# Layer 0 of a two-layer encoder on one core: attention softmax in spaced steps, the short conv's weights two units earlier, the first block modulated first, two plain units of the output projection, and large tiles at multiples of 64 bytes

## The chip, the cores and the metric

The kernel runs on one core of one Trainium2 chip. Its engines are TensorE (PE, matrix products, with its weight loads shown as PEld), VectorE (DVE), ScalarE (ACT), GpSimd (POOL) and SyncE (SP), which issues all transfers here. They share an on-chip memory (SBUF) and the accumulators of TensorE (PSUM). The metric is the device time of one execution in microseconds (us), lower is better.

## What is computed

A two-layer encoder on 256 positions of width 2048, all in float32:

```python
for l in range(2):
    mod = (silu(c) @ w_mod[l] + b_mod[l])            # 2048 x 12288 per layer
    shift_m, scale_m, gate_m, shift_f, scale_f, gate_f = mod in six parts of 2048
    h = layer_norm(x) * (1.0 + scale_m) + shift_m
    proj = h @ w_in[l]
    uv, q_c, kv_c, k_r, sb, sc, sh, ag = split(proj)  # widths 1024, 384, 256, 64, 512, 512, 512, 1024
    y_a = gmlp_mixer(uv, ...)                         # A: chunked spatial gating
    y_b = mla_mixer(q_c, kv_c, k_r, ...)              # B: latent attention, 4 heads, rotary key
    y_c = sb * causal_dwconv3(sc * sh)                # C: short gated conv
    y_d = silu(layer_norm(causal_dwconv31(glu(ag))))  # D: conv module, 31 taps
    y = concatenate([y_a, y_b, y_c, y_d]) @ w_out[l]
    x = layer_norm(ALPHA * x + (1.0 + gate_m) * y, ...)
    h = layer_norm(x) * (1.0 + scale_f) + shift_f
    y = conv_ffn(h, ...)                              # 2048 -> 2 x 5632 -> 2048
    x = layer_norm(ALPHA * x + (1.0 + gate_f) * y, ...)
```

## The kernel before

**Precision and pools.** Most large products are done in a faster format: ACT casts a weight tile to a high part `whi` (L382), DVE subtracts it from the raw one `wraw` to give a low part `wlo` (L383), activations are split in the same way (L402), and three products (high x high, low x high, high x low) take the place of one. Such weights are "split". In layer 0 the input projection and the later chunks of `w_out` use "plain" float32 weights `wexact` instead, which go straight from the transfer into a product, on more TensorE time and no ACT or DVE time. Tiles come from pools of a few buffers each.

**Order.** The Python program emits instructions in an order of its own, and a scheduler then orders each engine's queue by data, buffers and manual dependencies. `stream` (L331) loads one unit of weights, emits the products of the unit before, calls `pump` and takes `bg` steps from the list `background`. A `phase` sets how many modulation steps `pump` emits for one unit (`RATES`), and `STEPS` sets how many background steps there are. `None` entries in `background` are steps that emit nothing.

**Modulation.** `mod` is a matrix times one vector, done on DVE: each of its steps takes 1 MB of `w_mod` and one instruction over 128x2048 (L188 `wmod<-wmod,crep`, or L198 `macc<-wmod,cact,macc` for a gate). The first two of layer 0 (shift and scale) are made block by block in `first_mod_of`: a block is 128 of the 2048 channels, two such products, a small sum (`mod`, L1407) and one ACT instruction on `hF`, the transposed normalised input. The other ten come from the stream of steps through `pump`.

**Layer 0's mixers.** `normed_T` normalises `x` with two powers on POOL (L141, `rs_in`) and writes `hF` with 32 transposes (`ps_xT`, L1390). `by_blocks` then goes through the 16 blocks of 128 channels, as each is modulated, with the D, U and V columns, next the B columns (latents of the attention) and at last the C columns (short conv). `mix_d` puts the 31 taps of conv D into `background`: four ACT scalings `scaled` (L842) and one DVE addition (L843) each, then `norm_d`: mean over channels, centring (L862), variance, power on POOL (`rd`, L876), a diagonal `dgD` (L882), and TensorE's `ps_rD` that spreads it. `attend` turns the latents `lat` by transposes (`ps_q`, `ps_kv`, L1000), scales them on ACT into `qg` (L1006, L1009), makes the rotary key (`kc`, L1012, and the `rope` copies), the queries and keys with `wq` and `wkv`, the scores and softmax (L1084 to L1121), and the product with the values.

**Output projection.** `out_proj` takes 2048 output columns in three chunks, `CHUNKS = ((0, 1024), (1024, 512), (1536, 512))`, and the 16 row blocks of `w_out` in units; in the first chunk a unit is two row blocks. `o` are its accumulators; the rows come in the order a, b, c, d of the mixers' outputs `ya` to `yd`. In layer 0 the second and third chunk are plain, the first is split.

Of the kernel before, what the change touches and what calls it, by code (L numbers as in the profile page):

```python
# [35 lines left out]
    dict(B=1.2, C=2.4, out=1.6, up=0.7, down=0.7),  # L36
    dict(D=1.0, U=0.0, V=0.0, B=0.0, C=0.0, E=0.9, out=0.6, up=0.3, down=0.7),
# [3 lines left out]
    dict(B=1, C=4, up=2),  # L41
    dict(U=7, B=4, C=4, E=8, up=2),
]

# [38 lines left out]
def encoder_kernel(ctx: ExitStack, tc: tile.TileContext, A: dict, consts: bass.AP, out: bass.AP):  # L83
# [56 lines left out]
    def power(o, i):  # L140
        pool.tensor_tensor(out=o, in0=i, in1=mhalf[:, : i.shape[1]], op=ALU.pow)  # L141
# [6 lines left out]
    par = keep.tile([P, PARAMS], F32, name="par")  # L148
# [31 lines left out]
    MOD = {}  # L180
    order_dep = mybir.DependencyInfo(mybir.DependencyClass.NoSync, mybir.DependencyReason.DATA)

    def mod_block(l, m, kt, col):

        raw = raw_tile("wmod")
        c0 = m * D + kt * P
        nc.sync.dma_start(out=raw, in_=A["w_mod"].take(D, lambda a: a[l, :, c0 : c0 + P].T))
        i = dve.scalar_tensor_tensor(  # L188
            out=raw, in0=raw, scalar=1.0, in1=crep, op0=ALU.mult, op1=ALU.mult, accum_out=col
        )  # L190
        held(i, "mod")

# [8 lines left out]
    def gate_rows(l, m, acc):  # L201
# [34 lines left out]
        return [lambda q=q: part(q) for q in range(5)]  # L236
# [94 lines left out]
    def stream(load, products, bg=0, mods=True):  # L331
# [4 lines left out]
        if mods:  # L336
            pump()
# [201 lines left out]
    def run(g):  # L539
        units, load, products, end, bg = g  # L540
        for u in range(units):
            stream(lambda: load(u), lambda item, u=u: products(item, u), bg)
            pending.extend(postponed)
            postponed.clear()
# [3 lines left out]
    last_norm = [None, None]  # L548

    def rstd_of(stats, name, want_nmr):  # L550
# [4 lines left out]
        power(r[:, 0:1], r[:, 0:1])  # L555
# [31 lines left out]
    def out_proj(l, w, src, order, gate_of, name, post_g, post_b, before, then, plain=(), bg=0):  # L587
# [111 lines left out]
        for c0, width in CHUNKS:  # L699
# [11 lines left out]
            def load_unit(u, c0, width, nk, units, last):  # L711
# [3 lines left out]
                exact = c0 in plain  # L715
                parts = weights(w, kt, nk, c0, width, exact, spare)
                s4 = src[kt // 4]
# [24 lines left out]

            for u in range(units):
                stream(lambda: load(u), lambda item, u=u, unit=unit: unit(item, u), bg if c0 == 0 else 1, not last)

            def done(state=state, c0=c0, nk=nk, last=last):
# [7 lines left out]
                if last:  # L754
                    drain_background()
                for t in range(2):
# [14 lines left out]
    def mixers(l, w_in, Y, hF=None, first_mod=None):  # L771
# [7 lines left out]
        CLB = lambda j: pm[:, 149 + j : 150 + j]  # L779

# [35 lines left out]
        def conv_d(glu):  # L816
# [16 lines left out]
            def taps(k):  # L833
# [7 lines left out]
                for j in range(4):  # L841
                    act.activation(out=t[:, j, :n], in_=glu[:, j, :n], func=AF.Copy, scale=CW(k, j))  # L842
                dve.tensor_tensor(out=yd[:, :, 30 - k :], in0=yd[:, :, 30 - k :], in1=t[:, :, :n], op=ALU.add)  # L843
# [10 lines left out]
            background.append(lambda: norm_d(yd))  # L854

        def norm_d(yd):
            Y["d"] = slot("yd").rearrange("p (j s) -> p j s", j=4)
            ps = ms_tile("ps_mean")
            for j in range(4):
                mm(ps[:, :S], ones, yd[:, j, :], j == 0, j == 3)  # L860
            for j in range(4):
                dve.scalar_tensor_tensor(  # L862
                    out=yd[:, j, :], in0=ps[:, :S], scalar=-1.0 / W_G, in1=yd[:, j, :], op0=ALU.mult, op1=ALU.add
                )
            sq = [tmp_tile("sqD0"), tmp_tile("sqD1")]
            for b in range(2):
                act.activation(
                    out=sq[b].rearrange("p (j s) -> p j s", j=2), in_=yd[:, 2 * b : 2 * b + 2, :], func=AF.Square
                )
            ps = ms_tile("ps_var")  # L870
            for t in range(2):
                for j in range(4):
                    o = (j % 2) * S + t * P
                    mm(ps[:, t : t + 1], sq[j // 2][:, o : o + P], ones[:, 0:1], j == 0, j == 3)
            rd = smallp.tile([P, 4], F32, tag="rd", name="rd")
            dve.tensor_scalar(  # L876
                out=rd[:, 0:2], in0=ps[:, 0:2], scalar1=1.0 / W_G, scalar2=LN_EPS, op0=ALU.mult, op1=ALU.add
            )
            power(rd[:, 2:4], rd[:, 0:2])
            dg = tmp_tile("dgD")  # L880
            for t in range(2):
                dve.tensor_scalar(  # L882
                    out=dg[:, t * P : (t + 1) * P], in0=ident, scalar1=rd[:, 2 + t : 3 + t], scalar2=None, op0=ALU.mult
                )
            ps = ms_tile("ps_rD")
            mm(ps[:, :S], ones, dg[:, :S], True, True)
            for j in range(4):
                dve.tensor_tensor(out=yd[:, j, :], in0=yd[:, j, :], in1=ps[:, :S], op=ALU.mult)
            for j in range(4):
                act.activation(out=Y["d"][:, j, :], in_=yd[:, j, :], func=AF.Silu, scale=CG(j), bias=CLB(j))  # L890

# [60 lines left out]
        def mix_b(wide, narrow):  # L952
# [38 lines left out]
            postponed.append(lambda: attend(WQ, WKV, lat, q01, rr))  # L991

        def attend(WQ, WKV, lat, q01, rr):
# [32 lines left out]
            act.copy(rope[64:128, 3, :], ps[64:128, :S])  # L1026

            qn = slot("qn").rearrange("p (j s) -> p j s", j=4)
            for b in range(2):
# [5 lines left out]
                act.copy(qn[:, 2 * b : 2 * b + 2, :], ps.rearrange("p (j s) -> p j s", j=2))  # L1035
            for b in range(2):
# [11 lines left out]
            for b in range(2):  # L1048
# [11 lines left out]
                act.copy(kn[:, 2 * b : 2 * b + 2, :], ps.rearrange("p (j s) -> p j s", j=2))  # L1060
# [514 lines left out]
```

## Time and profile before

| what | value |
|---|---|
| three runs | 2245.35, 2253.36, 2249.52 us; median 2249.52 |
| profiled execution | 2243.58 us; span in the trace 2241.8 us |
| mean granted TensorE clock | 0.996 |
| busy: PE / weight loads / DVE / ACT / POOL | 2196.2 / 1801.8 / 1722.7 / 1097.4 / 29.2 us |
| read from device memory | 600.01 MB, 269 GB/s over the span |
| layer 0: first D product; first C products; end of C; end of `w_out`'s first chunk | 25.09; 204.80; about 304; about 364 us |

The profile is of one execution. A row of the timeline has start, duration, engine, source line, operation, output and inputs, shapes and count, and in brackets how long the engine was idle ahead of it and what released it. A slice has the busy time of each engine with its number of instructions, the clock granted to TensorE, the DMA engines' busy share and the data rate. In a row of groups the busy total and the mean in ns stand behind the bar, and then the idle time ahead.

### The profile page before, as it was taken

The page shows a single profiled execution, that of the slowest core. Times are in us where ns is not written, and L with a number is a line of the kernel's source. Part 1 is how long each engine was busy: PE and PEld are TensorE (multiplying, and loading weights), DVE is VectorE, ACT ScalarE, POOL GpSimd, SP SyncE. Part 2 cuts the span into 40 slices and gives each one's busy share as a digit, 9 for nine tenths or more (in the row PEclk, how much of TensorE's full clock was granted, in tenths as well). Part 3 has the DMA queues.
Part 4 walks back from the last instruction along what each step waited for, and adds up shares of the span by engine and source line. Part 5 has one row for each costly group of instructions (what it writes and reads, how often), then busy time and mean ns, then how long its engine had stood idle before and what let it go on. Part 6 is the DMA issues. An engine that isn't in the chain of part 4 may idle for free. (4 is left out here: it accounts for less than half of the span.)

```text
span 2241.8 us, 28321 instructions
## 1 busy us (share of the span) xinstructions
PE 2196.2 (98%) x10852; PEld 1801.8 (80%) x10852; DVE 1722.7 (77%) x2203; ACT 1097.4 (49%) x1683; POOL 29.2 (1%) x38
## 2 busy tenths in 40 slices
PE   8999989999999999999999999999999999999997
PEld 5876865488888888888877988868888888888886
DVE  5658887698988888988968987867775566565776
ACT  3136431555545454545556544555555555454453
POOL 0000000000000000000000000000000000000000
PEclk9999999999999999999999999999999999999999
DMA  9998879598988889888766656866665555555554
GB/s 393 408 359 314 318 295 417 227 338 312 329 322 312 334 314 329 316 321 329 288 240 247 211 173 238 295 221 244 244 228 186 188 188 190 189 193 199 188 190 148
DMA packets 93746, 603.96 MB, mean 269 GB/s; under 512 B 10533, under 2 KB 10661, under 8 KB 28581
## 3 DMA queue, kind: packets, MB, share of 16 engines
q1 hardware_dynamic: 93610, 602.15, 73.2%
q8 instruction: 85, 1.39, 0.2%
q14 instruction: 51, 0.42, 0.1%
HBM read 600.01 MB, written 2.10 MB: 269 GB/s over the span
## 5 line engine op out<-in xcount | busy, mean ns | idle before, releaser
L382 ACT CAST whi<-wraw 128x1024 fp32r<-128x1024 f32 (+1 forms) x612 | 638.0, 1046 | 693.0 <-PE g_c L111 208.1
L383 DVE TENSOR_TENSOR wlo<-wraw,whi 128x1024 fp32r<-128x1024 f32 (+1 forms) x612 | 736.0, 1215 | 287.0 <-ACT whi L382 280.5
L111 PE MATMUL v_c<-hT,whi 128*128 128x512 f32 x1408 | 490.4, 392 | 0.0
L111 PE MATMUL g_c<-hT,whi 128*128 128x512 f32 x1280 | 444.9, 391 | 0.0
L111 PE MATMUL v_c<-hT,wlo 128*128 128x256 f32 x1408 | 394.6, 280 | 0.0
L111 PE MATMUL d<-whi,a 128*128 128x512 f32 x1344 | 386.3, 389 | 0.0
L111 PE MATMUL g_c<-hT,wlo 128*128 128x256 f32 x1280 | 358.4, 280 | 0.0
L188 DVE SCALAR_TENSOR_TENSOR wmod<-wmod,crep 128x2048 f32<-128x2048 f32 x128 | 291.9, 2287 | 41.9 <-DMA wmod<-in_w_mod_dram 41.9
L111 PEld LDWEIGHTS v_c<-hT,whi 128*128 128x128 f32 x1408 | 263.4, 187 | 58.3
L111 PEld LDWEIGHTS d<-whi,a 128*128 128x128 f32 x1344 | 252.1, 188 | 52.4
L111 PEld LDWEIGHTS g_c<-hT,whi 128*128 128x128 f32 x1280 | 239.4, 187 | 52.7
L111 PEld LDWEIGHTS v_c<-hT,wlo 128*128 128x128 f32 x1408 | 266.1, 189 | 0.2
L111 PEld LDWEIGHTS g_c<-hT,wlo 128*128 128x128 f32 x1280 | 241.9, 189 | 0.1
L111 PE MATMUL d<-wlo,a 128*128 128x512 f32 x672 | 232.8, 389 | 0.0
L198 DVE SCALAR_TENSOR_TENSOR macc<-wmod,cact,macc 128x2048 f32<-128x2048 f32 x60 | 140.9, 2349 | 8.3 <-DMA wmod<-in_w_mod_dram 8.2
L111 PEld LDWEIGHTS d<-wlo,a 128*128 128x128 f32 x672 | 126.1, 188 | 26.2
L111 PE MATMUL o<-whi,a 128*128 128x512 f32 x352 | 100.9, 395 | 7.6 <-ACT whi L382 7.6
L402 DVE TENSOR_TENSOR a<-g,a 128x512 fp32r<-128x512 f32 x132 | 88.9, 686 | 0.1
L526 PE MATMUL first<-wexact,hN 128*128 128x512 f32 x192 | 85.7, 596 | 1.5 <-ACT hN L114 1.2
L111 PEld LDWEIGHTS o<-whi,a 128*128 128x128 f32 x352 | 66.5, 190 | 23.2 <-ACT whi L382 9.3
L401 ACT CAST a<-g 128x512 fp32r<-128x512 f32 x132 | 81.0, 613 | 8.2 <-PE d L111 4.8
L1353 DVE SCALAR_TENSOR_TENSOR u<-g,par,u 128x254 f32<-128x254 f32 (+1 forms) x176 | 74.3, 480 | 0.4 <-ACT u L114 0.2
(315 smaller groups left out, 2374.3 us busy)
## 6 DMA issues: line engine op xcount, KB each, us to landing
wmod<-in_w_mod_dram SPq DMA_DIRECT2D x192, 1024.0 KB, 6.7
wraw<-in_ffn_w_up_dram SPq DMA_DIRECT2D x168, 1024.0 KB, 5.1
wraw<-in_ffn_w_down_dram SPq DMA_DIRECT2D x88, 1024.0 KB, 5.0
wexact<-in_w_in_dram SPq DMA_DIRECT2D x64, 512.0 KB, 8.6
wraw<-in_w_out_dram SPq DMA_DIRECT2D x24, 1024.0 KB, 5.1
wraw<-in_w_in_dram SPq DMA_DIRECT2D x24, 1024.0 KB, 5.1
wexact<-in_w_out_dram SPq DMA_DIRECT2D x16, 512.0 KB, 12.9
wexact<-in_ffn_w_up_dram SPq DMA_DIRECT2D x16, 512.0 KB, 5.5
```

Of the source, the lines that this page charges most:

```text
L111: pe.matmul(o, lhsT, rhs, start=start, stop=stop, skip_group_check=True)
L188: i = dve.scalar_tensor_tensor(out=raw, in0=raw, scalar=1.0, in1=crep, op0=ALU.mult, op1=ALU.mult, accum_out=col)
L198: i = dve.scalar_tensor_tensor(out=acc, in0=w, scalar=col, in1=acc, op0=ALU.mult, op1=ALU.add)
L382: held(act.copy(hi[:, :m], r), "cast")
L383: i = dve.tensor_tensor(out=lo[:, :m], in0=r, in1=hi[:, :m].bitcast(F32), op=ALU.subtract)
L401: act.copy(hi, src)
L402: dve.tensor_tensor(out=lo, in0=src, in1=hi.bitcast(F32), op=ALU.subtract)
L526: i = pe.matmul(ps, hN[kt // 4][:, kt % 4, t * P : (t + 1) * P], parts[kt], start=kt == 0, stop=kt == KT - 1, skip_group_check=True,)
L1353: dve.scalar_tensor_tensor(out=u[:, sh:], in0=x[:, : S - sh], scalar=col(k, j), in1=u[:, sh:], op0=ALU.mult, op1=ALU.add)
```

## The change

All of it is for layer 0 unless said otherwise.

1. The first block goes first. Quarter 0 of the normalised input is transposed ahead of the mods, quarters 1 to 3 after blocks 0 to 2 are modulated. The first modulation product waits for the second power. 8 and 14 products of a constant with itself (`spare`) stand behind the two transposed tiles of quarter 0.
2. Attention is a generator whose steps are emitted a unit of C apart; scores of the first two groups come before either is turned (this order in layer 1 too). The taps' scalings on ACT stand behind the rope copies. Five more calls emit modulation steps within `attend`. `norm_d` is cut in five steps with empty steps between.
3. C's weights are loaded two units further ahead.
4. The first two units of `w_out`'s first chunk are plain. The background is no longer emptied before the output projection. `RATES` and `STEPS` change with it.
5. The tile `par` is padded from 866 to 880 floats, which moves all large tiles that are allocated behind it from 32 bytes past a multiple of 64 to a multiple of 64.

```diff
 RATES = [
-    dict(B=1.2, C=2.4, out=1.6, up=0.7, down=0.7),
+    dict(B=1.3, attend=1.3, C=1.9, out=1.0, out_next=2.3, out_last=0.0, up=0.7, down=0.7, down_next=0.7, down_last=0.0),
...
-    dict(B=1, C=4, up=2),
+    dict(B=1, C=6, out=1, up=2),
...
+PLAIN_UNITS = 2
...
-    par = keep.tile([P, PARAMS], F32, name="par")
+    par = keep.tile([P, -(-PARAMS // 16) * 16], F32, name="par")
...
+        lead = [lambda: None] if (l, m) == FIRST_GATE else []
+        return lead + [lambda q=q: part(q) for q in range(5)]
...
-    def run(g):
+    def run(g, ahead=0):
...
+        def get(u):
+            while len(loaded) < min(u + ahead + 1, units):
+                loaded.append(load(len(loaded)))
+            return loaded[u]
...
-                exact = c0 in plain
+                exact = c0 in plain or (bool(plain) and u < PLAIN_UNITS)
...
+            if c0 > 0:
+                phase(l, f"{stage}_last" if last else f"{stage}_next")
...
+        def more_mods():
+            pace["credit"] += RATES[l]["attend"]
+            rate, pace["rate"] = pace["rate"], 0.0
+            pump()
+            pace["rate"] = rate
...
-                    act.activation(out=t[:, j, :n], in_=glu[:, j, :n], func=AF.Copy, scale=CW(k, j))
+                    i = act.activation(out=t[:, j, :n], in_=glu[:, j, :n], func=AF.Copy, scale=CW(k, j))
+                    if attended:
+                        tc.add_manual_dep(i.ins, attended[0], order_dep, reason="the latents come first")
...
-                        background.extend([lambda: None] * 8)
+                        background.extend([lambda: None] * 12)
...
+            steps = norm_d(yd)   # now [mean, centred, variance, deviation, scaled]
+            if hF is not None:
+                steps = [lambda: None] + steps[:1] + [lambda: None] * 5 + steps[1:2] + [lambda: None] * 5 + steps[2:]
+            background.extend(steps)
...
+            def step():
+                for _ in steps:              # steps = attend(WQ, WKV, lat, q01, rr), a generator
+                    if hF is not None:
+                        postponed.append(step)
+                        return
...
+            p0 = softmax(0, 0)
+            p1 = softmax(1, 0)
+            yield
+            yield
+            yield
+            turned(p0, 0, 0)
+            p2 = softmax(1, 1)
+            yield
+            turned(p1, 1, 0)
+            yield
+            turned(p2, 1, 1)
+            yield
...
-                blocks[at["mods"]]()
+                modulated = blocks[at["mods"]]()
...
+                if at["mods"] in (2, 4, 6):
+                    quarter(at["mods"] // 2, modulated)
...
-        run(group(w_in, C_SC, 1024, f"C{l}", mix_ce, hF=hf, bg=STEPS[l]["C"]))
-        drain_background()
+        run(group(w_in, C_SC, 1024, f"C{l}", mix_ce, hF=hf, bg=STEPS[l]["C"]), 2)
...
+        def warm(i, n):
+            for _ in range(n):
+                j = pe.matmul(spare[:, :P], ident, ident, start=True, stop=True, skip_group_check=True)
...
+                if q == 0:
+                    warm(i, (8, 14)[t])
...
+                if kt == 0:
+                    tc.add_manual_dep(i.ins, powers, data_dep, reason="the power's operands share a port with this")
```

The order of the instructions shows three places where work moves. First, TensorE at the start of the program; `ps_xT` are the transposes of the normalised input, `D_c`, `U_c`, `V` the products of the first block, `spare` the products of the constant. Before:

```order
L111 MATMUL ps_c<-crow,ones 128x512 x4
L1390 MATMUL ps_xT<-cst,xn 128x128 x32
L111 MATMUL D_c_207<-hF_115,wexact 128x256 x2
L111 MATMUL D_c_208<-hF_115,wexact 128x256 x2
L111 MATMUL D_c_209<-hF_115,wexact 128x256 x2
```

And of the change:

```order
L113 MATMUL ps_c<-crow,ones 128x512 x4
L1471 MATMUL ps_xT<-cst,xn 128x128 x4
L1457 MATMUL spare<-cst 128x128 x8
L1471 MATMUL ps_xT<-cst,xn 128x128 x4
L1457 MATMUL spare<-cst 128x128 x14
L113 MATMUL D_c_140<-hF_115,wexact 128x256 x2
L1471 MATMUL ps_xT<-cst,xn 128x128 x4
L113 MATMUL D_c_141<-hF_115,wexact 128x256
L1471 MATMUL ps_xT<-cst,xn 128x128 x4
L113 MATMUL D_c_141<-hF_115,wexact 128x256
```

Eight transposes stand ahead of the first D product instead of 32, with 22 products of the constant; the other 24 transposes stand among the products.

Second, ACT behind the latents, where TensorE waits for `qg`; `rr` and `lat` belong to the latents' norm, `scaled` to the taps of conv D. Before:

```order
L114 ACTIVATE rr<-ss,rms_eps 128x2 x2
L842 ACTIVATE scaled<-gluD,par 128x238
L988 ACTIVATE lat_1026<-lat_1026,rr 128x256
L988 ACTIVATE lat_1027<-lat_1027,rr 128x256
L842 ACTIVATE scaled<-gluD,par 128x238
L842 ACTIVATE scaled<-gluD,par 128x237 x4
L842 ACTIVATE scaled<-gluD,par 128x236 x4
L842 ACTIVATE scaled<-gluD,par 128x235
L1006 ACTIVATE qg<-ps_q,par 128x256
```

And of the change:

```order
L116 ACTIVATE rr<-ss,rms_eps 128x2 x2
L1029 ACTIVATE lat_1060<-lat_1060,rr 128x256
L1029 ACTIVATE lat_1061<-lat_1061,rr 128x256
L1055 ACTIVATE qg<-ps_q,par 128x256
L1058 ACTIVATE qg<-ps_q,par 128x256
L1055 ACTIVATE qg<-ps_q,par 128x256
L1074 COPY rope<-ps_kr 64x256
L1075 COPY rope<-ps_kr 64x256
L864 ACTIVATE scaled<-gluD,par 128x248 x4
L864 ACTIVATE scaled<-gluD,par 128x247 x3
```

No tap stands between the latents and `qg` any more; where the tap of width 238 stood, that of width 248 follows now, behind the rope copies.

Third, TensorE at the end of C and the beginning of the output projection; `C_c` are the last products of the short conv's columns, `ps_rD` the spread reciprocal deviation of conv D, `o` the output projection. Before:

```order
L111 MATMUL ps_rD<-dgD,ones 128x256
L111 MATMUL C_c_1059<-hF_118,wexact 128x256
L111 MATMUL C_c_1060<-hF_118,wexact 128x256 x2
L111 MATMUL C_c_1059<-hF_118,wexact 128x256 x2
L111 MATMUL C_c_1060<-hF_118,wexact 128x256 x2
L111 MATMUL o_000_1671<-whi,a 128x512
L111 MATMUL o_001_1672<-whi,a 128x512
L111 MATMUL o_000_1671<-wlo,a 128x512
L111 MATMUL o_001_1672<-wlo,a 128x512
```

And of the change:

```order
L113 MATMUL o_010_1665<-wexact,ya 128x512
L113 MATMUL o_011_1666<-wexact,ya 128x512
L113 MATMUL ps_rD<-dgD,ones 128x256
L113 MATMUL o_000_1663<-wexact,ya 128x512
L113 MATMUL o_001_1664<-wexact,ya 128x512
L113 MATMUL o_000_1663<-wexact,ya 128x512
L113 MATMUL o_001_1664<-wexact,ya 128x512
L113 MATMUL o_010_1665<-wexact,ya 128x512
L113 MATMUL o_011_1666<-wexact,ya 128x512
L113 MATMUL o_010_1665<-wexact,ya 128x512
L113 MATMUL o_011_1666<-wexact,ya 128x512
L113 MATMUL o_000_1663<-whi,a 128x512
```

`ps_rD` has moved from ahead of the last C products to behind the first eight plain products of the output projection (the first two rows are the last of those eight), and eight more plain products stand ahead of the first split one.

On SP the order of the transfers is the same up to the middle of B, where two of `w_mod` come a step earlier. Behind B six of C's weight tiles stand in a row ahead of `wq` and `wkv`, where there were two, and the plain weights of `w_out`'s first unit stand behind five transfers of `w_mod`.

More of the change, by code (lines that the diff above doesn't have):

```diff
@@ L875, in norm_d @@
[L875 to L890, printed above, removed]
+            box = {}
+            def mean():
+                Y["d"] = slot("yd").rearrange("p (j s) -> p j s", j=4)
+                box["mean"] = ms_tile("ps_mean")
+                for j in range(4):
+                    mm(box["mean"][:, :S], ones, yd[:, j, :], j == 0, j == 3)
@@ L1114, in attend @@
[L1114 to L1121 removed]
+                return pt
@@ L1380, in normed_T, with quarter @@
             rs.append(r)
-        for q in range(4):
+        powers = last_power[0].ins.name
+        spare = acc_tile("spare")
+        def warm(i, n):
+            for _ in range(n):
+                j = pe.matmul(spare[:, :P], ident, ident, start=True, stop=True, skip_group_check=True)
+                tc.add_manual_dep(j.ins, i.ins.name, order_dep, reason="the transposes come first")
+        def quarter(q, after):
             for t, (mv, r) in enumerate(zip(mvs, rs)):
```

215 lines of the change are left out of this document (123 added, 92 removed).

## The prediction

> **What bounds the kernel now.** I read the page first, then the slices of the first 400 us, then what TensorE waits for there, and last its timeline at the places the change touches. The page says that TensorE is the bound of the whole.
>
> ```profile
> PE 2196.2 (98%) x10852; PEld 1801.8 (80%) x10852; DVE 1722.7 (77%) x2203; ACT 1097.4 (49%) x1683; POOL 29.2 (1%) x38
> ```
>
> Of 2241.8 us only 45.6 are idle on TensorE, so nothing is to be had but those, spells at half clock, and work taken off it. Slices of 20 us (busy time of PE, weight loads, DVE, ACT, POOL; granted clock; DMA share; GB/s) show where:
>
> ```profile
> 0.00:20.00 20.00, 11.13 (x24) 5.46 (x24) 12.38 (x20) 9.83 (x18) 3.62 (x10) 1.00 0.89 351
> 20.00:40.00 20.00, 19.45 (x72) 14.63 (x71) 11.36 (x13) 6.69 (x12) 0.00 (x0) 1.00 1.02 415
> 200.00:220.00 20.00, 16.24 (x65) 11.44 (x63) 14.89 (x15) 16.05 (x49) 2.44 (x3) 0.92 0.70 286
> 220.00:240.00 20.00, 19.48 (x82) 16.73 (x83) 18.55 (x17) 15.40 (x39) 0.00 (x0) 0.91 0.65 232
> 300.00:320.00 20.00, 12.75 (x46) 9.17 (x44) 19.60 (x30) 11.58 (x18) 0.00 (x0) 0.91 0.60 214
> 320.00:340.00 20.00, 16.64 (x68) 12.45 (x68) 19.34 (x21) 4.23 (x5) 0.00 (x0) 1.00 0.98 373
> ```
>
> Three stages of layer 0 hold TensorE's idle time that the change can reach: the start, the turn of the attention latents (200 to 220, clock 0.92), and the first chunk of the output projection (300 to 364), where DVE is busy 19.6 of 20. TensorE's waits up to 520 us name them (total, times, longest):
>
> ```profile
> PE o L111 <- ACT whi L382: 7.6, 4, 3.6
> PE ps_xT L1390 <- ACT xn L114: 5.7, 5, 3.1
> PE o L111 <- DVE wlo L383: 5.1, 6, 2.6
> PE ps_q L1000 <- ACT qg L1006: 3.2, 1, 3.2
> ...
> PE ps_kv L1000 <- ACT qg L1006: 0.3, 1, 0.3
> ```
>
> The first and third are the split of `w_out` into two halves (ACT casts, DVE subtracts) before its products; 7.6 + 5.1 = 12.7 us. I cost the three stages one after the other, each in the times of the profiled execution before.
>
> **The start: -3.0 us.** The first block's modulation and first D products, the same products of the second block, a later block's pair, the two powers on POOL, a modulation product, and eight transposes at full speed:
>
> ```profile
> 24.43 0.60 ACT L114 ACTIVATE hF<-hF,mod 128x256 f32<-128x256 f32 x1
> 25.09 5.70 PE L111 MATMUL D_c<-hF,wexact 128*128 128x256 f32 x16
> 34.07 3.62 PE L111 MATMUL D_c<-hF,wexact 128*128 128x256 f32 x16
> 41.20 0.60 ACT L114 ACTIVATE hF<-hF,mod 128x256 f32<-128x256 f32 x1 [8.58 <-DVE mod L1407]
> 47.86 3.19 PE L111 MATMUL D_c<-hF,wexact 128*128 128x256 f32 x14
> 10.03 0.55 POOL L141 TENSOR_TENSOR rs_in<-rs_in,mhalf 128x1 f32<-128x1 f32 x1 [8.99 <-DVE rs_in L554]
> 12.82 2.56 POOL L141 TENSOR_TENSOR rs_in<-rs_in,mhalf 128x1 f32<-128x1 f32 x1 [2.24 <-DVE rs_in L554]
> 29.49 2.29 DVE L188 SCALAR_TENSOR_TENSOR wmod<-wmod,crep 128x2048 f32<-128x2048 f32 x1 [1.46 <-DMA wmod<-in_w_mod_dram]
> ...
> 437.40 1.04 PE L571 MATMUL ps_xT<-cst,xn 128*128 128x128 f32 x8
> ```
>
> Today all 32 transposes come ahead of the first product at 25.09, and its 16 records take 5.70 us where the same 16 take 3.62 at 34.07: TensorE starts slow, 2.1 us lost, although the clock column reads 1.00. In the changed kernel the first modulation product waits for the second power, which then runs alone: 0.55 instead of 2.56, ended at 13.4. Two 2.29 us products follow (18.1 with small steps), then the 0.60 activation: the first block is ready at about 19.3 instead of 25.0, an estimate. But TensorE has 22 dummy products in front: 8 at the slow rate, four transposes, 14 more, and all this from 13.9, when the first four transposes are through. Their time is an estimate: a 128x256 product is two records, so 0.45 at the rate of 34.07 and 0.71 at that of 25.09, and a 128x128 one half as much. Eight at 0.36 to 0.45 are about 3.4, fourteen at 0.23 are 3.2, and the four transposes 0.5: 21.0. If all 22 run at 0.45, it is 24. From 25.1 to 21 is 4.1, and nearly all of the 2.1 goes too; back come 24 transposes moved into the stream (1.04 for eight: 3.1) and, a choice, some 0.3 of waits for their copies: -4.1 - 2.1 + 3.1 + 0.3 = -2.8, or -3 in round numbers. Bounds are -5 (the start at 19.3) and +0.5 (all slow). What hides the later blocks' readiness is their slack: the block of 41.20 is ready at 41.8 and used at 47.86. Without that cover each late block would cost its 2.29 us product.
>
> On those two powers the Trainium skill (SBUF — State Buffer, section on SBUF's two separate sides) says that a DVE operation with two SBUF inputs and a GpSimd operation that reads SBUF take a shared port pair as an exclusive lock for the whole instruction. The 2.56 us beside a DVE product against 0.55 alone agree; by that rule the later power on the conv norm, which the change puts among DVE's products, could cost up to 2 us more, inside the spread below.
>
> **The latents: -4.0 us.** The end of the first C products, the two groups of turns, the last products on the queries, ACT in between, and the clock:
>
> ```profile
> 204.80 7.07 PE L111 MATMUL C_c<-hF,wexact 128*128 128x256 f32 x32
> 215.52 0.77 PE L1000 MATMUL ps_q<-cst,lat 128*128 128x128 f32 x4 [3.21 <-ACT qg L1006]
> 218.00:220.00 2.00, 1.94 (x6) 0.50 0.00 0
> 220.52 6.99 PE L111 MATMUL ps_qn<-qg,wq 128*128 128x256 f32 x24 [0.58 <-DVE kvr L1017]
> 227.35 1.46 PE L111 MATMUL ps_qr<-qg,wq 128*128 128x256 f32 x6
> 211.19 3.92 ACT L842 ACTIVATE scaled<-gluD,par 128x238 f32<-128x238 f32 x10
> ```
>
> ACT has ten scaled taps (3.92 us) ahead of `qg`, and TensorE waits 3.21 for it, with 0.58 and 0.3 more behind it: 4.1. A stretch at clock 0.50 follows: 24 records take 6.99 where six take 1.46 (24 would take 5.84), 1.1 lost, and the four or so microseconds before it ran at half, 2.1 lost: 3.2. With the taps ordered behind the rope copies ACT has only the two latent scalings ahead; one new wait of about 1.8 stays, since the first turn of the latents now stands ahead of C's products. So 4.1 - 1.8 + 3.2 = -5.5 at its best. Some is given back: the taps displaced here stand later on DVE, where the turn of the probabilities and the mean then wait, 1.5 (between 0 and 3). That leaves -4.0 at the end of C (bounds -2.5, -5.5). The two yields between the softmax steps only separate work that TensorE has anyway. C's weights two units earlier cost nothing on TensorE: its C products run without a wait today; the price is on the queue, where `wq` and `wkv` come after them, with over 10 us of C products as cover.
>
> Of that half clock the Trainium skill (TensorE: Matmul & The Clock Gate, Part 1) says that the array falls back to half rate after an idle window of about 3.4 us and wants as long of steady work to return. The 0.50 after the 3.21 wait agrees. It speaks against the next step of this change, which puts a longer wait into the output projection: by it that wait costs an estimated 1.7 us of lost work, half of the 3.4.
>
> **DVE falls behind.** From the first `kc` to the end of `dgD` DVE has, today:
>
> ```profile
> 216.39:300.38 83.99, 82.42 (x374) 67.66 (x374) 66.55 (x85) 32.80 (x78) 0.70 (x1) 0.96 0.75 288
> 299.90 0.48 DVE L882 TENSOR_SCALAR dgD<-cst,rd 128x128 f32<-128x128 f32 x2 [0.88 <-POOL rd L141]
> L188 DVE SCALAR_TENSOR_TENSOR wmod<-wmod,crep 128x2048 f32<-128x2048 f32 x11 | 24.9, 2286 | 0.0
> L843 DVE TENSOR_TENSOR convD<-convD,scaled 128x940 f32<-128x940 f32 (+9 forms) x10 | 11.1, 1109 | 0.5 <-ACT scaled L842 0.5
> L402 DVE TENSOR_TENSOR a<-yb,a 128x512 fp32r<-128x512 f32 x2 | 1.4, 690 | 1.8 <-ACT a L401 1.8
> 300.97 3.19 PE L111 MATMUL C_c<-hF,wexact 128*128 128x256 f32 x14
> ```
>
> 66.6 us busy in 84. By the order of the changed kernel the same stretch holds 13 more taps (1.11 each: 14.4), 4 more modulation products (2.29: 9.2), the short conv's ten steps and two sums, which used to come later (four 128x512 operations at 0.69, eight half as large at 0.4: 6.0), and three fewer casts' remainders (-2.1): +27.5, so 94.1. `kc` comes at about 215.5 and DVE has no gap left, so `dgD` ends at 309.6 without any wait, and with the few that stay (2.5, like those for ACT's `scaled` and `a` now) at about 312. It ended at 300.4.
>
> **The output projection's first chunk: -4.9 us.** What it takes now, its first and last products, the clock after its first wait, four plain products (eight records), the split of one unit on DVE, and a slice late in the program where TensorE is full of split products:
>
> ```profile
> 303.97:364.17 60.20, 47.42 (x189) 35.78 (x189) 56.77 (x63) 20.82 (x27) 0.00 (x0) 0.97 0.92 362
> 307.76 0.73 PE L111 MATMUL o<-whi,a 128*128 128x512 f32 x2 [3.60 <-ACT whi L382]
> 310.00:312.00 2.00, 2.00 (x6) 0.50 0.61 250
> 363.33 0.84 PE L111 MATMUL o<-whi,a 128*128 128x512 f32 x3
> 404.62 3.60 PE L111 MATMUL o<-wexact,yd 128*128 128x512 f32 x8
> 325.08 2.35 DVE L383 TENSOR_TENSOR wlo<-wraw,whi 128x1024 fp32r<-128x1024 f32 x2
> ...
> 2000.00:2020.00 20.00, 20.00 (x90) 16.57 (x89) 11.19 (x11) 10.50 (x12) 0.00 (x0) 1.00 0.59 207
> ```
>
> Eight units took 60.2 us with TensorE 47.4 busy, and 12.8 idle. At full clock 90 recorded split products fill 20 us, 0.22 each, and a few records may be missing; I take 0.227, which gives 5.46 us for the 24 of a unit, 43.7 for eight. The other 3.7 of the 47.4 went to half clock, as at 310, behind two waits. In the changed kernel two units are plain: 16 products each of 0.86 (four in 3.60, less the overlap at its end), 13.8 for both instead of 10.9, with nothing on ACT or DVE. From C's end at 300.0: eight plain products to 306.9; then `ps_rD` waits for `dgD` until 312.6, 5.7; eight more 6.9, slowed by 1.5 after that wait (like the half clock after the 3.60); six split units 32.8; 1.5 of waits for their casts, since DVE has 2.35 of subtracting and at most one modulation product of 2.29 a unit, which is under 5.46. Sum 55.3, end at 355.3 against 364.2, and 4.0 of that was there before: -4.9.
>
> **The rest: 0.** The second chunks are plain already, the modulation moved out of the first chunk is hidden there (2.3 products of 2.29 a unit against 6.9 on TensorE). Layer 1 has the new softmax order alone, and TensorE's waits on that are below 1 us in the list of waits. That all large tiles start 32 bytes further on, at multiples of 64, moves nothing on the bound: 0, between -1 and +1, as the transfers into the shifted tiles run at 415 GB/s in the second slice.
>
> Sum: -3.0 - 4.0 - 4.9 = -11.9. The profiled execution took 2243.58 (span 2241.8), so it would be 2231.7; the median of three is 2249.52, which gives 2237.6, **2238**.
>
> **The rivals.**
> `dgD` in time (0.18): if DVE's steps are shorter in their new places or the scheduler puts some of the mods behind it, `ps_rD` does not wait, and 5.7 + 1.5 go too: -19, 2230. For: 82.4 of 84 us TensorE is busy there, so DVE's work has no earlier limit; against: it needs 6 of DVE's 94 us.
> The start's gain is lost (0.14): the dummies run slow and the interleaved transposes wait; then -9, 2241.
> DVE later still (0.13): 6 us more of waits among taps, POOL's power and PSUM give -6, with the start's loss -3: within 0.3%.
> Slower (0.17): the modulation products run out of data. 21 of them stand between `kc` and `dgD`, and each needs its own 1 MB. Today they don't wait (idle 0.0 in their row) at 288 GB/s, but the same stretch must now carry 4 MB of them and some 3 MB of plain weights more, about 370 GB/s, and the `w_out` weights stand behind five such transfers on SP. At the 1.46 us wait of the start's row each, 21 x 1.46 = 30.7 us is added ahead of `dgD`, and TensorE stands behind it with only eight products: -11.9 + 30.7 = +18.8, 2268. It decides from 0.57 us a product (11.9 / 21), and is measurable from 0.89. Against it stand 415 GB/s in the second slice.
>
> **How the numbers follow.** The forecast has 0.38. Of cases in order, 0.38 + 0.18 + 0.14 are faster by over 0.3% (6.7 us, about what a measurement here can tell from no change): 0.70; within it 0.13; slower 0.17. The range runs from 2226 (no wait for `dgD`, start at its good bound, less a few us of scatter between executions) to 2251 (all bounds at their bad end); what is left out is the slower case beyond its onset and a little below.
>
> **What would show it.** First D product at 21 (24 if the dummies are slow); second power at 0.55; no wait over 2 us before `ps_q`, clock not at 0.50 at 218; DVE without a gap from `kc` on and `dgD` at about 309 on the new clock (312 less the start's 3); a wait of 5 to 6 us before `ps_rD` with a dip in the clock; first chunk ended near 352. The forecast is wrong if `ps_rD` does not wait, or DVE waits for `wmod`, or time moves in layer 1.

## The result, and the profile after

Six runs of the changed kernel have a median of 2236.66 us (2234.39 to 2239.71), six of the kernel before beside them 2245.62 (2243.77 to 2253.36): ratio 0.9956, 95% interval 0.9943 to 0.997. In a second set of runs it was 2236.35 (nine runs) against 2245.88, ratio 0.995 (0.9932 to 0.9969). So it is faster by 9.0 and 9.5 us by the medians, 9.9 and 11.2 by the ratios, where 11.9 were forecast. The profiled execution has a span of 2232.3 us against 2241.8; the profile of the second set (called the second profile below) has 2237.3.

What TensorE waits for up to 520 us in the changed kernel (total, times, longest):

```profile
PE o L113 <- DMA wexact<-in_w_out_dram: 4.6, 4, 3.0
PE ps_rD L113 <- DVE dgD L919: 3.9, 1, 3.9
...
PE ps_mean L113 <- DVE convD L867: 2.0, 1, 2.0
PE ps_xT L1471 <- ACT xn L116: 1.7, 1, 1.7
PE ps_q L1049 <- ACT lat L1023: 1.0, 1, 1.0
```

The waits for `whi`, `wlo` and `qg` are gone. That for `dgD` (0.2 before) has grown, and those before `ps_mean` and for `lat` are new; all three were forecast. The first row is new and was not: plain weights of `w_out` that have not landed. TensorE's timeline of the changed kernel at the ends of the stages:

```profile
20.71 1.03 PE L113 MATMUL D_c<-hF,wexact 128*128 128x256 f32 x4
120.34 7.07 PE L113 MATMUL E<-hF,wexact 128*128 128x256 f32 x32
296.50 8.83 PE L113 MATMUL o<-wexact,ya 128*128 128x512 f32 x16 [0.33 <-DMA wexact<-in_w_out_dram]
309.25 1.19 PE L113 MATMUL ps_rD<-dgD,ones 128*128 128x256 f32 x2 [3.92 <-DVE dgD L919]
351.91 7.03 PE L113 MATMUL o<-wexact,ya 128*128 128x512 f32 x16
384.78 5.37 PE L113 MATMUL o<-wexact,ya 128*128 128x512 f32 x8 [2.98 <-DMA wexact<-in_w_out_dram]
414.02 1.04 PE L582 MATMUL ps_xT<-cst,xn 128*128 128x128 f32 x8
```

And the same ends before (the start of the projection stands in the prediction: 307.76 less its wait of 3.60):

```profile
123.74 7.07 PE L111 MATMUL E<-hF,wexact 128*128 128x256 f32 x32
365.14 9.60 PE L111 MATMUL o<-wexact,ya 128*128 128x512 f32 x22
420.07 1.28 PE L571 MATMUL ps_xT<-cst,xn 128*128 128x128 f32 x8
```

And in the second profile of the changed kernel:

```profile
120.57 7.07 PE L113 MATMUL E<-hF,wexact 128*128 128x256 f32 x32
297.95 7.11 PE L113 MATMUL o<-wexact,ya 128*128 128x512 f32 x16
353.42 7.03 PE L113 MATMUL o<-wexact,ya 128*128 128x512 f32 x16
415.70 1.04 PE L582 MATMUL ps_xT<-cst,xn 128*128 128x128 f32 x8
```

| stage that ends | before | after | lead | gained in the stage | gained, second profile | forecast |
|---|---|---|---|---|---|---|
| start (an early group of E products) | 123.74 | 120.34 | -3.40 | -3.40 | -3.2 | -3.0 |
| attention and C | 304.16 | 296.17 | -7.99 | -4.59 | -3.0 | -4.0 |
| first chunk of `w_out` | 365.14 | 351.91 | -13.23 | -5.24 | -5.5 | -4.9 |
| second and third chunk | 420.07 | 414.02 | -6.05 | **+7.18** | **+7.4** | 0 |
| the rest, to the end of the span | 2241.8 | 2232.3 | -9.5 | -3.45 | -0.1 | 0 |

At 352 us the changed kernel leads by 13.2 us, all three forecast terms within 0.6 (within 1.0 in the second profile); then it loses 7.2 of it in a stage costed at nothing. Of the last row, 1.4 us lie at the turn to the FFN and 2.1 in layer 1; the second profile has no such gain.

### The profile page after: what moved, and what is told of

Its sections match the earlier page's. It is cut to its first block, busy times and chain, and to the rows that moved or that the text cites. A ratio compares the mean times of both kernels' runs of the same rounds, so it can differ in the third digit from the quotient of the medians.

```text
span 2232.3 us, 28361 instructions
## 1 busy us (share of the span) xinstructions
PE 2197.6 (98%) x10880; PEld 1800.1 (81%) x10880; DVE 1715.7 (77%) x2197; ACT 1093.6 (49%) x1677; POOL 25.8 (1%) x38
## 5 line engine op out<-in xcount | busy, mean ns | idle before, releaser
L113 PE MATMUL o<-whi,a 128*128 128x512 f32 x320 | 90.5, 390 | 0.0
L113 PEld LDWEIGHTS o<-whi,a 128*128 128x128 f32 x320 | 60.0, 188 | 12.9 <-issue 0.5
```

The costliest lines, as they stand in the source:

```text
L113: pe.matmul(o, lhsT, rhs, start=start, stop=stop, skip_group_check=True)
```

## The experiments

Each is the changed kernel with one edit, if nothing else is said, and runs beside the kernel before. Where an edit lies in `RATES`, only the entries that differ are printed.

**Fewer modulation steps in the second chunk.**

```diff
-out=1.0, out_next=2.3, out_last=0.0
+out=1.0, out_next=1.3, out_last=1.0
```

> The changed kernel with 1.3 modulation steps a unit in the second chunk of w_out instead of 2.3, and 1.0 in the third instead of none; everything else as in the change. Theory V (volume): the 4.6 us that TensorE waits there for plain weights, and the half clock after the 2.98 us one, come from 3.3 MB a unit at about 420 GB/s, 7.8 us or more for 6.9 us of products. Then the waits for wexact fall under 1 us, TensorE goes from the end of the first chunk to the end of the third in 55 us instead of 62.1, and the execution is 4 to 7 us faster than the changed kernel (ratio to before about 0.993). Theory H (head of the line): what is lost is the idle stretch of the queue from 336 to 345 us, in which SP waits 8.1 us to place the first plain tile; that stays, so the waits stay at 3 us or more, and the time within 2 us of the changed kernel (0.9955).

2238.14 us, ratio 0.9945 (0.9925 to 0.9964). The waits for `wexact` are gone, and the two chunks' products run without a gap from 350.70 to 405.8; then TensorE waits for the next stage (its timeline):

```profile
414.52 1.97 PE L582 MATMUL ps_xT<-cst,xn 128*128 128x128 f32 x8 [8.73 <-ACT xn L116]
```

The steps in the third chunk stand on DVE among the steps of the layer norm that makes `xn`. Theory V is right on the waits, which go although the DMA share from 340 to 350 us stays at 0.56 here, and wrong on the gain: the volume was moved to where DVE ends last.

**Three steps ahead of the chunk's first weights.**

```diff
-out_next=2.3
+out_next=1.55
...
+            if l == 0 and stage == "out" and 0 < c0 and not last:
+                for _ in range(3):
+                    next(mods, None)
```

> The changed kernel with three of the modulation steps of w_out's second chunk issued ahead of that chunk's first weights, and 1.55 a unit instead of 2.3 behind that; the sum is the same. Theory H: the queue no longer stands idle from 336 to 345, since its raw buffers can take transfers while the plain tile waits; DMA share in 340 to 350 rises from 0.5 to over 0.8, the waits for wexact go, 5 to 7 us faster than the changed kernel (0.993). Theory V: volume from 336 to 400 is unchanged and the pool of four raw buffers holds the queue as before; a gain of under 3 us.

2232.69 us, ratio 0.9919 (0.9896 to 0.9942), some 4 us faster than the changed kernel by medians that stand on different chips; its trace is 5.0 ahead at the end of the projection. In the changed kernel SP's queue waits for a buffer that the split products still read (its waits from 320 to 400 us), and the slices show what that costs (PE, weight loads, DVE, ACT, POOL, clock, DMA share, GB/s):

```profile
SPq L370 <- PE o L113: 8.1, 1, 8.1
```

```profile
340.00:350.00 10.00, 10.00 (x46) 8.29 (x45) 5.48 (x7) 2.00 (x2) 0.00 (x0) 1.00 0.51 185
350.00:390.00 40.00, 35.76 (x83) 15.42 (x82) 33.12 (x39) 0.00 (x0) 0.00 (x0) 0.96 1.02 418
```

The same slices, and the same wait of SP, with the three steps ahead:

```profile
SPq L370 <- PE o L113: 11.0, 3, 9.1
```

```profile
340.00:350.00 10.00, 10.00 (x46) 8.28 (x45) 5.27 (x7) 2.01 (x2) 0.00 (x0) 1.00 0.97 379
350.00:390.00 40.00, 38.72 (x95) 17.58 (x94) 33.00 (x39) 0.00 (x0) 0.00 (x0) 1.00 1.01 407
```

The transfers run at half their rate for 10 us because a plain tile stands at the head of the line, and then TensorE starves at 418 GB/s. With the raw transfers put ahead, SP still waits 9.1 us for that buffer, but the share rises from 0.51 to 0.97, the waits for `wexact` fall from 4.6 to 1.4, and the projection's end comes at 409.0 instead of 414.0. Both theories hold a part: 3.3 MB a unit is too much once the head start is lost.

**Fewer steps in C, more in the first chunk.**

```diff
-C=1.9, out=1.0
+C=1.4, out=1.5
```

> The changed kernel with 1.4 modulation steps a unit of C instead of 1.9 and 1.5 a unit of w_out's first chunk instead of 1.0 (four of them moved behind the norm of conv D). Theory: DVE is what ends last before ps_rD, at 2.3 us a step, so dgD comes about 9 us earlier relative to C's end, the 3.9 us wait and the slow clock behind it go (5.5 us in the first chunk); the split units have 2.35 + 3.4 of DVE work in 5.46, so about 0.3 us a unit comes back as waits for whi and wlo, and the second chunk starts with less arrears. Net 2 to 5 us faster than the changed kernel. Rival: the split units become DVE-bound and give all of it back, within 1 us.

2237.42 us, ratio 0.9947 (0.9931 to 0.9964): no gain. The wait for `dgD` is gone, split units wait 4.2 for `whi` and 2.1 for `wlo`, and the end of the third chunk still comes 7 us earlier. What took it back is one modulation step that had become late, on DVE behind the last norm; TensorE waits 4.57 us for it, and its products behind that wait are slow (timelines of DVE and PE):

```profile
409.61 2.27 DVE L191 SCALAR_TENSOR_TENSOR wmod<-wmod,crep 128x2048 f32<-128x2048 f32 x1
...
412.70 2.08 PE L530 MATMUL first<-wexact,hN 128*128 128x512 f32 x2 [4.57 <-ACT hN L116]
```

**Both together, milder.**

```diff
-C=1.9, out=1.0, out_next=2.3
+C=1.65, out=1.25, out_next=1.55   # and the three steps ahead
```

> The changed kernel with three modulation steps ahead of the first weights of w_out's second chunk, 1.55 a unit behind them, and 1.65 a unit of C with 1.25 a unit of the first chunk instead of 1.9 and 1.0 (two steps moved behind conv D's norm). Theory: dgD comes 4.6 us earlier, so of the 5.8 us that TensorE waits for it in the version with the three steps ahead about 1 stays, with no half clock behind it, and DVE still has 2.35 + 2.9 in the 5.46 of a split unit: 2 to 5 us faster than that version (2228 to 2231, ratio 0.990). Rival: the two steps come back as waits of the split units for whi and wlo, or of the first ffn_up group for hN, and it lies within 1 us of that version (2232).

2232.07 us, ratio 0.9925 (0.9903 to 0.9947). The rival holds: it is within 1 us of the version with the three steps alone. No wait for `dgD` is left, but 3.2 for a plain weight, 2.9 for `whi` and 0.5 for `wlo` came. Both versions beat the changed kernel by some 4 us.

**No plain units in the first chunk.**

```diff
-PLAIN_UNITS = 2
+PLAIN_UNITS = 0
```

> The changed kernel with no plain units in w_out's first chunk (all eight split); the rest of the change stays. Theory (the forecast's term): TensorE has 2.9 us less to do, but waits 7 to 12 us for whi and wlo at the beginning, since DVE is behind by 10 us there; the first chunk ends 3 to 7 us later and the whole is 2 to 6 us slower than the changed kernel (ratio 0.9975). Rival: the wait before ps_rD (3.9 to 6.1 us) stood in the same place and covers the split, so it is within 1 us or faster by up to 3.

2240.68 us, ratio 0.9964 (0.995 to 0.9977). In the trace the two slices from C's end to the chunk's end are, here and in the changed kernel:

```profile
299.18:353.30 54.12, 47.42 (x196) 37.91 (x195) 51.36 (x65) 23.07 (x29) 1.15 (x1) 0.91 0.85 318
...
296.17:351.91 55.74, 51.50 (x179) 35.19 (x179) 49.12 (x63) 19.44 (x25) 1.07 (x1) 0.91 0.83 326
```

All split, the chunk takes 1.6 us less, since a wait of 5.2 for `whi` stands where the wait for `dgD` and the dearer products stood; C before it ends 3.0 later (a wait of 3.3 instead of 2.0 before `ps_mean`, with three small ones behind it). The end of the projection is 414.29 against 414.02. So the plain units by themselves are worth 0.3 to 1.4 us against the first profile of the changed kernel, and -1.4 to -0.1 against the second (353.42 and 415.70): these traces show no difference. The medians say 4, and the chip is an unlikely reason, since the kernel before is not slower on this one (its lower group of runs lies at 2242 to 2246 us here and at 2243 to 2248 beside the second set); where those 4 us lie is not shown. The plain units are not what shortened the chunk in the trace. What else did was not tried by itself: the background is no longer emptied ahead of the chunk, and it has 1.0 modulation steps a unit for 1.6. The lower rate alone is a doubtful reason, since with 1.5 a unit (and fewer in C, above) the chunk ended at 349.79.

**Taps free of the latents.** The two lines that hold `scaled` behind the rope copies are taken out.

> The changed kernel without the order that keeps conv D's scalings on ACT behind the rope copies; the spaced attention steps stay. Theory: this order is what took the latents' wait away, so a wait of 2 to 4 us for qg on ACT is back at 210 us, with a dip of the clock to 0.5 for 3 to 4 us; but DVE then gets taps earlier and dgD comes earlier by as much, so the 3.9 us before ps_rD shrink: net 0 to 3 us slower than the changed kernel. Rival: the interleaving of C's products with the turns alone covers ACT's delay; then no wait over 1 us, and with dgD earlier the kernel is 1 to 4 us faster than the change.

2238.45 us, ratio 0.9956 (0.994 to 0.9972), 2 us above the changed kernel's median on the same chip, but the runs overlap (2234.66 to 2242.35 against 2234.77 to 2240.34), so that this is not clear of their scatter. The wait for `qg` is back; in its timeline, the 24 records of the attention's queries behind it take 5.72 instead of 5.34:

```profile
214.10 1.11 PE L1047 MATMUL ps_q<-cst,lat 128*128 128x128 f32 x4 [4.26 <-ACT qg L1053]
221.47 5.72 PE L113 MATMUL ps_qn<-qg,wq 128*128 128x256 f32 x24
```

No wait for `dgD` is left in layer 0. So the order of the taps is what removes the wait at `qg`, and it trades 4.3 us and a slow clock there for 3.9 to 6.1 us at `dgD`. What it keeps of the trade is open: the first chunk ends at 353.37 here, and at 351.91 and 353.42 in the two profiles of the changed kernel.

**The old start.** All quarters first, no dummies, no wait for the power; the diff shows the quarters alone.

```diff
-        quarter(0, None)
+        for q in range(4):
+            quarter(q, None)
...
-                if at["mods"] in (2, 4, 6):
-                    quarter(at["mods"] // 2, modulated)
```

> The changed kernel with the old start: all quarters transposed ahead of the first product, no dummy products, no wait for the power. Theory: the start's 3.40 us come from here alone, so the first D product is at 25.1 again with its 16 records at 5.7 us, everything behind is 3.4 later up to the output projection, and the execution 3 to 3.5 us slower than the changed kernel (0.9970). Rival: DVE and the queue, not TensorE, pace the stage from B on, so that the later start is caught up by 200 us and the execution is under 1 us slower.

2241.64 us, ratio 0.9956 (0.9938 to 0.9974). The first D products start at 25.81 with 16 records at 5.74, and the power of the gMLP norm comes at 162.65 instead of 158.49: 4.2 us, which are not caught up (median 5 us above the changed kernel's).

**No dummies.**

```diff
-warm(i, (8, 14)[t])
+warm(i, 0)
```

> The changed kernel without the 22 dummy products at the start. Theory: the first block is modulated at 19.0 us, so the first D product starts at about 19 instead of 20.7, but at the slow rate: its stretch of 16 records takes 5 to 5.7 us instead of 3.6 and the gain of 1.7 is given back; the stage before B within 0.7 us and the whole within 1 us of the changed kernel. Rival: the transposes among the products and the wait for the second block make the start stall again at the slow rate, 2 to 3 us slower. Other rival: the slow rate ends at the same moment whatever stands there, and 1.5 us are gained.

2240.09 us, ratio 0.9959 (0.9944 to 0.9974). The first D products in its timeline:

```profile
19.07 1.22 PE L113 MATMUL D_c<-hF,wexact 128*128 128x256 f32 x2 [2.07 <-ACT hF L116]
20.08 1.92 PE L1471 MATMUL ps_xT<-cst,xn 128*128 128x128 f32 x8
21.79 4.67 PE L113 MATMUL D_c<-hF,wexact 128*128 128x256 f32 x14
```

It starts 1.6 earlier at half the rate, and is 0.9 behind by the gMLP norm (0.7 against the second profile): the dummies gain that much there. The median's 3.5 is more than the trace shows up to the projection, whose end, at 415.59, lies with those of the changed kernel (414.02 and 415.70); where the rest lies is not shown, and as with the split units the chip is an unlikely reason.

**The addresses.** Twice the changed kernel with the tile `par` at its old width, with the changed kernel itself beside the second, and the kernel before with the padding alone.

```diff
-    par = keep.tile([P, -(-PARAMS // 16) * 16], F32, name="par")
+    par = keep.tile([P, PARAMS], F32, name="par")
```

> The changed kernel with the parameter tile at its old width, so that all large tiles start 32 bytes past a multiple of 64 again; the order of instructions is the same on every engine. Theory of the forecast: no effect, within 1 us of the changed kernel, no stage moved by over 0.5 us in the trace, transfers at 415 GB/s as before. Rival: the addresses are worth the 2.1 us that layer 1 gained and part of the 5.2 us of the first chunk; then 2 to 4 us slower than the changed kernel (0.9970).

> The kernel with the parameter tile at its old width once more. Theory A: most runs again at 2245 or 2254, and if the profiled one is among them, its extra 8 or 16 us lie in stages where TensorE has no spare time, spread over many instructions or in one place that the trace names. Theory C: it runs like the changed kernel beside it, within 2 us.

> The changed kernel as it is, beside the next ones on one chip. Theory A (addresses): the padding of the parameter tile takes away a slower course of execution that the kernel at its old addresses has in most runs (2253 us median against 2238 in its fastest), so this one stays between 2234 and 2240 in all its runs. Theory C (the chip): the slower course belongs to the chip or the hour; then this one too shows runs at 2245 and 2254.

> The kernel before with one thing of the change: the parameter tile padded, so that all large tiles start at multiples of 64 bytes; nothing else moves. Theory A (addresses): at the old addresses some executions have 2% slower products in the ffn_up stage of layer 0, of layer 1 or of both, about 6 to 8 us each; padded, all runs lie between 2241 and 2248, none at 2250 or above, median about 2243, 1 to 4 us under the kernel before (ratio 0.9985). Theory N: the slower course comes from the new order together with the old addresses, and the kernel before has its runs at 2251 to 2259 for another reason; then they stay in the padded one as well, as often as without it (11 of 29 beside the last runs).

| kernel | runs | times, us | ratio to before |
|---|---|---|---|
| changed, old addresses | 12 | 2 at 2238, 2 at 2245 to 2246, 8 at 2253 to 2254; median 2253.34 | 0.9996 (0.9976 to 1.0016) |
| the same, other chip | 12 | 3 at 2237 to 2238, 8 at 2246 to 2248, 1 at 2254; median 2246.75 | 0.9986 (0.9968 to 1.0004) |
| changed | 9 | 2234.77 to 2240.34, median 2236.35 | 0.995 (0.9932 to 0.9969) |
| before, padded | 12 | 2242.53 to 2246.85, median 2244.69 | 0.9981 (0.9967 to 0.9995) |
| before, beside the last | 27 | 13 at 2242 to 2246, 13 at 2250 to 2255, one at 3709 (not in the ratios) | 1 |

Theory A holds for the times: the order of instructions is the same with and without the padding, and only unpadded kernels have runs 8 or 16 us above their fastest. The second unpadded profile is such a run (span 2251.8), the first is not (2235.8). The same 50 us of ffn_up in each, the one of 2235.8 first, and the products with `whi` (duration min, median, max):

```profile
470.00:520.00 50.00, 50.00 (x290) 44.07 (x289) 45.92 (x53) 26.17 (x37) 0.00 (x0) 1.00 0.88 329
L113 PE MATMUL g_c<-hT,whi x1280: 390/391/403, 468.8 to 1962.3; 128*128 128x512 f32 x183
```

```profile
470.00:520.00 50.00, 50.00 (x285) 43.36 (x284) 44.42 (x51) 25.41 (x36) 0.00 (x0) 1.00 0.86 320
L113 PE MATMUL g_c<-hT,whi x1280: 387/398/403, 469.0 to 1977.9; 128*128 128x512 f32 x183
```

TensorE is full at clock 1.00 in both, but makes 285 products instead of 290, 398 ns each instead of 391. This 2% lasts through ffn_up of both layers, 8 us each (but for 580 to 600 us, where the products of `v_c` have 391 in this trace and 398 in the other); at 920 us, in ffn_down, the products keep 389. Times 8 us above the lowest would be those with one such layer. That reading is an inference, as is that the 2250 to 2255 us of the kernel before have the same cause; that they vanish with the padding is measured. The dear products themselves are not bound to the old addresses. The kernel before, padded, has them in the same 50 us and up to 590, and the changed kernel has them in layer 1 (`U_c`, columns of the input projection) in its second profile but not in its first:

```profile
470.00:520.00 50.00, 50.00 (x285) 43.33 (x285) 44.24 (x48) 25.90 (x38) 0.00 (x0) 1.00 0.90 322
L111 PE MATMUL g_c<-hT,whi x192: 389/398/404, 477.4 to 590.4; 128*128 128x512 f32 x192
```

```profile
L113 PE MATMUL U_c<-hT,whi x64: 391/391/391, 1234.1 to 1256.0; 128*128 128x512 f32 x64
L113 PE MATMUL U_c<-hT,whi x64: 395/398/404, 1236.6 to 1258.9; 128*128 128x512 f32 x64
```

What the traces show of the old addresses alone is a whole stage of them. Why products are dearer in some executions and not in others, and what the address has to do with it, stays open.

## Why the prediction was right, and where it was not

**The start** was right: second power at 0.55, first D product at 20.71 for 21, -3.40 for -3.0. The old start costs it again.

```profile
12.83 0.55 POOL L143 TENSOR_TENSOR rs_in<-rs_in,mhalf 128x1 f32<-128x1 f32 x1 [2.24 <-DVE rs_in L565]
```

**The latents** were right: clock 1.00 from 200 to 240, a new wait of 0.96 before the first turn (1.8 forecast), given back 2.04 before `ps_mean` (1.5 forecast); -4.59 for -4.0, and -3.0 in the second profile, where the products behind that wait of 2.04 were slow (`ps_mean` at 3.65 instead of 1.97). The slices:

```profile
200.00:220.00 20.00, 19.04 (x88) 14.81 (x87) 3.76 (x6) 11.52 (x35) 1.63 (x3) 1.00 0.93 377
220.00:240.00 20.00, 20.00 (x92) 15.84 (x91) 19.53 (x18) 17.02 (x43) 0.00 (x0) 1.00 0.38 127
```

**DVE behind** was right in its end, with two small errors that cancelled: 94.1 us of work and 2.5 of waits were forecast from `kc` to `dgD`, and the window has 92.1 and 5.4 (DVE is the third figure)

```profile
211.63:309.11 97.48, 91.32 (x400) 70.98 (x399) 92.10 (x116) 56.62 (x136) 1.07 (x1) 0.98 0.79 308
```

with `dgD` ended at 309.1 for 309. TensorE's wait was 3.92 here and 6.10 in the second profile; in the first one the slow clock fell on the eight products ahead (8.83 instead of 7.11), which is 1.7 of the 2.2 by which the wait was shorter.

**The first chunk** ended at 351.9 for 352, but its reason was not shown: "two units are plain" was the step, and without them it ends within 1.4 us of the same moment. The term was right in size, and what stands behind it is open. Its parts missed and cancelled: slow products cost 3.9 us (8.83 and 9.15 for 7.03 each) where 1.5 were forecast, the wait was 3.9 for 5.7, and the 1.5 of waits for casts did not come. The end before was read too early, too: the row at 363.33 was cut short by its window, and the chunk ended at 365.14, not at 364.2; the same sum from there gives -5.8.

**"The rest: 0" is the step that failed**, twice. The second chunk's modulation was called hidden because 2.3 products of 2.29 us on DVE fit in 6.9 us of TensorE. DVE was the wrong resource: 2.3 MB of `w_mod` and 1 MB of weights a unit take 3.3 x 1.05 MB / 0.418 = 8.3 us of the queue, and the queue came into the chunk late, having stood 8.1 us behind a buffer. It cost 7.2 us, of which 4.6 are waits and some 1.8 half clock behind the longest of them. And the addresses were given 0 between -1 and +1, on the ground that transfers ran at the same rate; the effect is on products, in other executions than the one profiled. Against its own kernel the padding is worth 4.3 us of the kernel before's time on its chip (ratio 0.9981; 6.1 by the medians) and 10 us and more of the changed one's.

So 2238 was close because errors met: the order of the work gave less than the -11.9 (7 to 8 us, across chips: 2244.69 of the padded kernel before to 2236.35, or 0.995 over 0.9981), and the padding the rest. The gain of 2.1 us in layer 1, which the prediction named as a sign of being wrong, is in no term, and none is needed: the second profile is 1.1 longer there than the kernel before. One slice in both, the first profile ahead:

```profile
1300.00:1310.00 10.00, 10.00 (x48) 7.97 (x48) 9.28 (x22) 4.07 (x7) 0.00 (x0) 1.00 0.30 106
...
1300.00:1310.00 10.00, 8.92 (x36) 6.64 (x37) 7.32 (x15) 4.61 (x8) 0.00 (x0) 0.83 0.32 105
```

None of the rivals came. That of slower had the right resource, transfers, in the wrong stage: no `wmod` wait stands between `kc` and `dgD`, but plain weights wait a stage later.

## What to carry to other kernels

Work moved off one stage must be costed in the stage that takes it on every resource it uses, transfers too: megabytes a unit over the rate that the queue has shown, and what stands at the queue's head when they are issued. A profile is one execution: an edit of addresses may leave it alone and still move the distribution of times, so compare distributions, not medians alone. Before a term is credited to an edit, undo that edit alone; here the plain units gave at most 1.4 of the stage's 5.2 us in the traces.

## What the runs showed of the hardware

Products of one shape, at a granted clock of 1.00 and with TensorE full, took 391 ns in some executions of one program and 398 in others. For a whole stage of some 470 us the traces show this only with the large tiles 32 bytes past a multiple of 64; for shorter spells (192 products of `g_c` to 590 us, 64 of `U_c`) they show it at multiples of 64 too.

The same short wait (2.1 us in layer 1) was followed by a dip of the clock to 0.83 in one execution and by none in another, 1.5 us or more apart at the end; the Trainium skill (TensorE: Matmul & The Clock Gate, Part 1) says that the window that decides is free-running, so that the count of slow products differs from run to run, and these two profiles agree. But the idle window of about 3.4 us that the prediction takes from that section of the Trainium skill is longer than the waits here: slow products followed waits of 2.0, 2.1 and 3.2 us, and the measurement decides.
